# Gate-weight loads of an FFN asked for one unit earlier in a two-layer encoder trunk

## The chip, the cores and the metric

The kernel runs on one core of a Trainium2 chip. The metric is the device time of one execution in microseconds (us). The inputs and the output lie in HBM, and all arithmetic is float32, with each large operand split into a high and a low part.

## The reference

Two layers over 1024 rows of width 1024. Each layer is a token mixer (latent attention in layer 0, differential attention in layer 1) and a SwiGLU block, each followed by a layer norm over a scaled residual:

```
h = x
for i in range(DEPTH):                       # DEPTH = 2
    ...                                      # mix = attention of layer i
    h = layernorm(ALPHA * h + mix)
    gate, up = split(h @ w_gu[i])            # w_gu: 1024 x 5632
    h = layernorm(ALPHA * h + (silu(gate) * up) @ w_down[i])   # w_down: 2816 x 1024
```

The change lies in the first half of the SwiGLU block: the products of `h` with `w_gu`.

## The kernel before, in words

The function `ffn` is called once for each layer. Its first half multiplies the activations with the gate and up weights in 22 units (`NFF`) of one 128-column block of `w_gu` each. The two units of a pair (even and odd number) make the gate and the up half of one hidden block. A product of a unit is a 2x2 block product done with seven block multiplications instead of eight, named "1" to "7". So each unit needs sums and differences of its four weight blocks a11, a12, a21 and a22.

**A unit's weights.** `load(n)` asks the SP queue for the 1 MB of unit n (L563) into a tile `gr` of a pool of six large buffers (`big`). The same six buffers also hold `pg` (early results), `hp` and `sh` (hidden blocks on their way to HBM). `prepare(n, pr)` makes the operand of product `pr`: VectorE (DVE) forms the sums in place (L585: a21 += a22; L587: a11 = a21 - a11; L589: a12 -= a11; L593: a scratch tile `s`), ScalarE (ACT) casts to the high part (L514), and DVE or GpSimd (POOL) subtracts to get the low part (L515). The result is an operand tile `op_g` that TensorE (PE) reads.

**A unit's products.** `consume(n, pr)` issues 12 matmuls (L551) into a PSUM bank: `ga` for products 1 and 2, `gb` for 6, 7 and 4, `gc` for 5 and 3. Products 6, 7 and 4 of a unit add up in the same `gb` bank one after the other, and DVE reads the bank between them (L633 after 6, L637 after 7, L643 after 4). So the matmuls of product 7 wait for L633 of the same unit, and those of product 4 for L637. The rest (L635, L639, L641, L645) adds `gc`, and L663 and L664 multiply into `hp`. POOL then forms `sh` from `hp` (L668 to L671), and two stores (L674, L675) send both to HBM.

**Units 0 to 5** (`npre = 6`) are the units prepared in advance: their products 1 and 2 run early (`gates`, from a half-size load `gp`, L569), and the results `pg` of units 2 to 5 are stored to HBM (L682) and fetched back into `tmp` (L655) when the unit's other products run. Units 0 and 1 read `pg` directly, so that buffer is held until both are finished.

**Order.** The list `stream` names the (unit, product) steps; each turn prepares the step four places ahead and then consumes one. A unit's first `prepare` also asks for later units' weights (the lines that the change touches). A scheduler then fixes each engine's instruction order, and decides which of the six buffers each tile gets. Each engine works through its queue in that order and does not pass an instruction that waits. The SP queue holds the weight loads, the `pg` stores and fetches, and the `hp` and `sh` stores, in one order.

Below, (2,7) means product 7 of unit 2. In names such as `gr0_5`, the first number is the layer, the second the unit.

Of the kernel before, what the change touches and what calls it, by code (L numbers as in the profile page):

```python
# [42 lines left out]
def trunk(  # L43
# [66 lines left out]
    def big_tile(name, dt=F32R):  # L110
        return big.tile([P, 2, 1024], dt, tag="big", name=name)
# [396 lines left out]
    def op_unit(src, eng, name, tags=("wh", "wl"), pool=None):  # L508

        tag = tags[turns["op"] % len(tags)]  # L510
        turns["op"] += 1
        where = wp if tag in ("wh", "wl") else pool
        t = where.tile([P, 2, 512], F32R, tag=tag, name=f"op_{name}", bufs=6 if pool is where else 3)
        turns["hi"] = A.copy(t[:, 0], src).ins  # L514
        turns["last"] = eng.tensor_tensor(t[:, 1], src, f32(t[:, 0]), ALU.subtract).ins  # L515
        return t
# [4 lines left out]
    def ffn(side, xo, xst, pending, layer, x_src, x_dst, lng, lnb, next_x, spare=()):  # L521
# [15 lines left out]
        npre = 6  # L537
# [21 lines left out]
        def load(n):  # L559
            if n in r or n >= NFF:  # L560
                return
            r[n] = big_tile(f"gr{layer}_{n}", F32).rearrange("p a (b c) -> p (a b) c", b=2)
            nc.sync.dma_start(r[n], w_gu[layer, order[n]])  # L563
# [11 lines left out]
        def prepare(n, pr):  # L575


            if n not in begun:
                begun.add(n)
                load(n + 1)  # L580
                if n < npre - 1:
                    load(n + 2)
            a11, a12, a21, a22 = (r[n][:, i] for i in range(4))
            if pr == ("5" if n < 2 else "6"):
                V.tensor_tensor(a21, a21, a22, ALU.add)  # L585
            if pr == ("3" if n < 2 else "6"):
                V.tensor_tensor(a11, a21, a11, ALU.subtract)  # L587
            if pr == "3":
                V.tensor_tensor(a12, a12, a11, ALU.subtract)  # L589
            s3 = None  # L590
            if pr == "7":
                s3 = wp.tile([P, 2, 512], F32, tag="wr", name=f"s3_{layer}_{n}", bufs=2)[:, 0]
                V.tensor_tensor(s3, a22, a11, ALU.subtract)  # L593
            src, eng = {
                "1": (a11, G), "2": (a12, G), "6": (a11, V), "7": (s3, G), "5": (a21, V), "4": (a22, G),
                "3": (a12, V),
            }[pr]
            eng = V if n < 2 else eng
            ops[n, pr] = op_unit(src, eng, f"g{layer}_{n}_{pr}")
# [118 lines left out]
        for u in stream[:2]:  # L718
            prepare(*u)
# [3 lines left out]
        for u in stream[2:ahead]:  # L723
            prepare(*u)
# [4 lines left out]
        for i, u in enumerate(stream):  # L729
            if i + ahead < len(stream):  # L730
                prepare(*stream[i + ahead])
            consume(*u)
            if i % 5 == 0 and 40 <= i < 40 + 5 * len(spare):
                spare[i // 5 - 8]()
# [835 lines left out]
```

## Time and profile before

| what | us |
|---|---|
| three timed runs | 2275.31, 2277.39, 2277.57 |
| median | 2277.39 |
| profiled execution, its own time | 2276.84 |
| profiled execution, span from first to last instruction | 2275.1 |
| PE busy | 2238.8 (98% of the span) |
| DVE busy | 1569.9 (69%) |
| loads `gr<-in_w_gu` | 44 of 1 MB, median 6.8 from issue to landing |

A row of a timeline reads: start in us from the span's beginning, duration, engine, line, operation, names (output <- inputs, without numbers), shapes, count, and in brackets the idle time before it and what ended it. A row of waits reads: who waited, for whom, us in total, times, longest. A row of the chain of waits reads: start, duration, what. "DMA to landing" is the time from the issue of a transfer to its completion.

The stretches of interest are the starts of the main loop in the two layers: about 490 to 525 us in layer 0 and 1675 to 1710 us in layer 1.

### The profile page before, as it was taken

To read this page: it belongs to the slowest core of one execution; us is meant where nothing else is said; L and a number is where in the kernel's file an instruction comes from. 1 tells how busy PE (TensorE), PEld (TensorE's weight loads), DVE (VectorE), ACT (ScalarE), POOL (GpSimd) and SP (SyncE) were. 2 spreads that over 40 slices of the span, in tenths; PEclk is the share of its full clock that TensorE was granted. 3 is DMA by queue.
4 is the path that set the end of the run, shared out by engine and by line. 5 is a ranking of instruction groups with operands and counts; after the bars stand their busy time and mean duration, and the time that the engine had idled before them with its cause. 6 is when DMAs were issued, how large, how long until landed. Compare 5 with 4: busy or idle time off the path is not lost.

```text
span 2275.1 us, 31209 instructions
## 1 busy us (share of the span) xinstructions
PE 2238.8 (98%) x11410; PEld 1915.3 (84%) x11410; DVE 1569.9 (69%) x2848; ACT 1022.1 (45%) x2115; POOL 869.2 (38%) x693
## 2 busy tenths in 40 slices
PE   8999999999999999999999999999999999999998
PEld 8899998887888888888889898987778888888886
DVE  5676665696666667878576667677786656658878
ACT  4455664342333333445465656555432333334444
POOL 2232341113444444656333534322014444445551
PEclk9999999999999999999999999999999999999999
DMA  5010115443535338454311212054343223238453
GB/s 203 14 35 31 51 61 188 145 156 103 183 128 195 125 130 324 176 199 148 103 44 32 70 33 67 20 202 167 111 171 117 92 102 107 100 124 311 164 180 149
DMA packets 110443, 287.77 MB, mean 126 GB/s; under 512 B 8513, under 2 KB 30657, under 8 KB 99793
## 3 DMA queue, kind: packets, MB, share of 16 engines
q1 hardware_dynamic: 105872, 275.35, 34.2%
q0 software_dynamic: 4416, 10.42, 1.7%
q8 instruction: 90, 1.47, 0.3%
q14 instruction: 65, 0.52, 0.1%
HBM read 204.47 MB, written 77.07 MB: 124 GB/s over the span
## 4 chain that ended last, share of the span: by engine, by line
PE 87%; DVE 6%; DMA 3%; issue 2%; ACT 1%; POOL 1%; SPq 0%; DVEq 0%; POOLq 0%; ACTq 0%
PE gb L551 14%; PE gc L551 10%; PE ga L551 8%; PE dw L843 6%; PE zp_a L417 4%; PE s_a L219 4%; PE s_b L219 3%; PE dv L843 3%; PE bp L143 3%; PE bp L145 3%; PE dx L843 3%; PE bp L144 3%; PE dy L843 2%; PE o_a L262 2%; PE o_b L262 2%
## 5 line engine op out<-in xcount | busy, mean ns | idle before, releaser
L514 ACT CAST op_g<-gr 128x512 fp32r<-128x512 f32 x240 | 146.8, 621 | 378.6 <-PE gb L551 185.3
L515 POOL TENSOR_TENSOR op_g<-gr,op_g 128x512 fp32r<-128x512 f32 x104 | 145.7, 1406 | 248.7 <-ACT op_g L514 144.5
L515 DVE TENSOR_TENSOR op_h<-rh,op_h 128x512 fp32r<-128x512 f32 x152 | 169.5, 1144 | 48.3 <-ACT op_h L514 48.3
L551 PE MATMUL ga<-xh_m,op_g 128*128 128x512 f32 x512 | 168.3, 389 | 0.0
L514 ACT CAST op_h<-rh 128x512 fp32r<-128x512 f32 x152 | 92.6, 620 | 152.0 <-PE dx L843 50.4
L843 PE MATMUL dw<-op_w_t,op_h 128*128 128x512 f32 x660 | 151.6, 390 | 0.6 <-DVE op_h L515 0.6
L843 PEld LDWEIGHTS dw<-op_w_t,op_h 128*128 128x128 f32 x660 | 123.6, 188 | 26.8 <-DVE op_h L515 1.4
L515 POOL TENSOR_TENSOR op_w_t<-tt,op_w_t 128x512 fp32r<-128x512 f32 x66 | 101.8, 1551 | 84.5 <-ACT op_w_t L514 83.0
L227 ACT ACTIVATE l_b<-l_b,mx_b 128x256 f32<-128x256 f32 (+7 forms) x128 | 99.4, 777 | 66.8 <-DVE mx_b L222 65.3
L515 DVE TENSOR_TENSOR op_g<-gr,op_g 128x512 fp32r<-128x512 f32 x136 | 112.6, 832 | 16.9 <-ACT op_g L514 16.6
L515 POOL TENSOR_TENSOR op_g<-s,op_g 128x512 fp32r<-128x512 f32 x40 | 55.1, 1376 | 179.5 <-ACT op_g L514 171.4
L551 PE MATMUL gb<-t3h_f,op_g 128*128 128x512 f32 x352 | 117.9, 397 | 5.5 <-DVE tmp L633 5.5
L843 PE MATMUL dx<-op_w_b,op_h 128*128 128x512 f32 x528 | 121.1, 390 | 0.8 <-DVE op_w_b L515 0.8
L1367 POOL TENSOR_SCALAR l_b<-l_b,rb,cst 128x128 f32<-128x128 f32 (+3 forms) x64 | 52.6, 821 | 179.2 <-DVE rb L1366 171.8
L843 PEld LDWEIGHTS dx<-op_w_b,op_h 128*128 128x128 f32 x528 | 98.9, 188 | 22.4 <-DVE op_w_b L515 1.7
L551 PE MATMUL gb<-t4h_f,op_g 128*128 128x512 f32 x352 | 115.7, 390 | 1.3 <-DVE tmp L637 1.3
L551 PE MATMUL gc<-b22h_f,op_g 128*128 128x512 f32 x352 | 115.8, 390 | 0.8 <-DVE tmp L641 0.6
L551 PE MATMUL gb<-t2h_f,op_g 128*128 128x512 f32 x352 | 115.7, 390 | 0.4 <-DVE op_g L515 0.4
L551 PE MATMUL gc<-t1h_f,op_g 128*128 128x512 f32 x352 | 115.9, 390 | 0.0
L551 PEld LDWEIGHTS ga<-xh_m,op_g 128*128 128x128 f32 x512 | 96.2, 188 | 19.9
L143 PE MATMUL bp<-xT_f,h_wb 128*128 128x512 f32 x256 | 100.8, 394 | 0.1
L145 PE MATMUL bp<-xT_f,l_wb 128*128 128x512 f32 x256 | 100.7, 393 | 0.0
(391 smaller groups left out, 6753.5 us busy)
## 6 DMA issues: line engine op xcount, KB each, us to landing
gr<-in_w_gu SPq DMA_DIRECT2D x44, 1024.0 KB, 6.8
rh<-h_dr SPq DMA_DIRECT2D x28, 1024.0 KB, 4.9
h_dr<-sh SPq DMA_DIRECT2D x22, 1024.0 KB, 4.9
h_dr<-hp SPq DMA_DIRECT2D x22, 768.0 KB, 4.1
tt<-in_w_dn SPq DMA_DIRECT2D x44, 256.0 KB, 6.3
wo_dr<-op_pwo SPq DMA_DIRECT2D x16, 512.0 KB, 3.4
z<-xs_dr SPq DMA_DIRECT2D x16, 512.0 KB, 8.2
rw_b<-in_w_dn SPq DMA_DIRECT2D x8, 1024.0 KB, 7.7
```

Source lines behind the costliest of these rows:

```text
L143: T.matmul(ps_out, lh, rh, start=(i == 0), stop=False)
L144: T.matmul(ps_out, lh, rl, start=False, stop=False)
L145: T.matmul(ps_out, ll, rh, start=False, stop=(i == n - 1))
L219: T.matmul(s[:, :w], lh, rh[:, ks], start=(j == 0), stop=(j == len(q_pass) - 1))
L227: ends["exp"] = A.activation(l[:, :n], l[:, :n], AF.Exp, bias=mx, scale=-1.0, accum_out=sm).ins
L262: T.matmul(po[:, c], a, b[:, j % 2, c], start=st, stop=sp_, skip_group_check=True)
L417: T.matmul(m, a[:, h, :], self.wo[h][w][:, c], start=(start and h == heads[0] and a is oh and w == 0), stop=(stop and h == heads[-1] and a ...
L514: turns["hi"] = A.copy(t[:, 0], src).ins
L515: turns["last"] = eng.tensor_tensor(t[:, 1], src, f32(t[:, 0]), ALU.subtract).ins
L551: i = T.matmul(o, w[:, a, kc], x[b][:, k, :], start=(first and k == 0 and (a, b) == (0, 0)), stop=(k == 3 and a == 1), skip_group_check=Tr ...
L843: T.matmul(o, h[:, a, c], w[:, b_], start=(first and (a, b_) == (0, 0)), stop=(last and a == 1), skip_group_check=True,).ins for a, b_ in ...
L1367: G.tensor_scalar(l1[:, :n], l1[:, :n], r[:, 1:2], nlam, ALU.mult, ALU.mult)
```

## The change

When unit n is first prepared, the kernel before asks for unit n+1, and for n+2 while n is below 5. The kernel after asks for n+1 and n+2 always, and for n+3 while n is below 4.

```
             if n not in begun:
                 begun.add(n)
                 load(n + 1)
-                if n < npre - 1:
-                    load(n + 2)
+                load(n + 2)
+                if n < npre - 2:
+                    load(n + 3)
```

A unit already asked for isn't loaded again. So units 3 to 6 are now asked for when the unit three before them begins instead of two, and from unit 7 on each load is asked for two units ahead instead of one. The number of loads stays the same. After the change the kernel has one line more, so that L585 of before is L586 there, L633 is L634, L637 is L638, and so on.

Since each tile takes the buffer that the scheduler finds free, the places of the loads and the buffers move. On the SP queue in layer 0, before (from `gr0_3` on; `pg_dr` is the HBM copy of the early results):

```order
L563 DMA gr0_3_5604<-in_w_gu 128x2048
L563 DMA gr0_4_5736<-in_w_gu 128x2048
L682 DMA pg_dr0_5320<-pg0_4_5501 128x2048
L655 DMA tmp0_2_5830<-pg_dr0_5320 128x1024
L655 DMA tmp0_3_5925<-pg_dr0_5320 128x1024
L563 DMA gr0_5_5845<-in_w_gu 128x2048
L674 DMA h_dr0_0_5309<-hp0_0_5757 128x3x512
L675 DMA h_dr0_0_5309<-sh0_0_5818 128x4x512
L563 DMA gr0_6_5940<-in_w_gu 128x2048
```

And the same place now:

```order
L563 DMA gr0_3_5583<-in_w_gu 128x2048
L563 DMA gr0_4_5606<-in_w_gu 128x2048
L683 DMA pg_dr0_5320<-pg0_4_5501 128x2048
L563 DMA gr0_5_5738<-in_w_gu 128x2048
L656 DMA tmp0_2_5832<-pg_dr0_5320 128x1024
L656 DMA tmp0_3_5927<-pg_dr0_5320 128x1024
L675 DMA h_dr0_0_5309<-hp0_0_5759 128x3x512
L563 DMA gr0_6_5847<-in_w_gu 128x2048
L676 DMA h_dr0_0_5309<-sh0_0_5820 128x4x512
```

The load of unit 5 stands ahead of the two fetches of `tmp` and takes the buffer of `pg0_4` (released by that tile's store) instead of that of `gr0_2` (released by the last step of unit 2). The load of unit 6 stands one place earlier and takes the buffer of `pg0_0` instead of that of `hp0_0`.

On DVE in layer 0, before, from the reading of unit 1's bank on:

```order
L633 TENSOR_TENSOR tmp0_1_5766<-pg0_0_5321,gb0_1_5765 128x512
L635 TENSOR_TENSOR tmp0_1_5766<-tmp0_1_5766,gc0_15_5668 128x512
L635 TENSOR_TENSOR tmp0_1_5766<-tmp0_1_5766,gc0_13_5684 128x512
L593 TENSOR_TENSOR s3_0_4_5960<-gr0_4_5736 128x512
L637 TENSOR_TENSOR tmp0_0_5703<-pg0_0_5321,gb0_0_5702 128x512
```

The three sums of unit 5 follow twelve rows further on, before:

```order
L663 TENSOR_TENSOR hp0_0_5757<-pg0_0_5321 128x512
L585 TENSOR_TENSOR gr0_5_5845<-gr0_5_5845 128x512
L587 TENSOR_TENSOR gr0_5_5845<-gr0_5_5845 128x512
L589 TENSOR_TENSOR gr0_5_5845<-gr0_5_5845 128x512
L633 TENSOR_TENSOR tmp0_2_5830<-tmp0_2_5830,gb0_2_5829 128x512
```

And now, from the same reading of unit 1's bank on:

```order
L634 TENSOR_TENSOR tmp0_1_5768<-pg0_0_5321,gb0_1_5767 128x512
L586 TENSOR_TENSOR gr0_5_5738<-gr0_5_5738 128x512
L636 TENSOR_TENSOR tmp0_1_5768<-tmp0_1_5768,gc0_15_5670 128x512
L588 TENSOR_TENSOR gr0_5_5738<-gr0_5_5738 128x512
L594 TENSOR_TENSOR s3_0_4_5960<-gr0_4_5606 128x512
L636 TENSOR_TENSOR tmp0_1_5768<-tmp0_1_5768,gc0_13_5686 128x512
L638 TENSOR_TENSOR tmp0_0_5705<-pg0_0_5321,gb0_0_5704 128x512
L590 TENSOR_TENSOR gr0_5_5738<-gr0_5_5738 128x512
L640 TENSOR_TENSOR tmp0_0_5705<-tmp0_0_5705,gc0_05_5636 128x512
L638 TENSOR_TENSOR tmp0_1_5768<-pg0_0_5321,gb0_1_5767 128x512
L665 TENSOR_TENSOR hp0_0_5759<-tmp0_0_5705 128x512
L515 TENSOR_TENSOR op_g0_2_5_5784<-gr0_2_5581,op_g0_2_5_5784 128x512
```

The three sums of unit 5 have moved from just ahead of the first reading of unit 2's bank (`tmp0_2`) to between the readings of units 0 and 1. In layer 1 the first of them stands one place earlier still, ahead of the reading of unit 1's bank. The matmuls of PE stand in the same order as before up to the first ones of (5,5) in both layers.

## The prediction

> **What bounds the kernel now.** I read the page first, then the waits of PE, the chain of waits around the two starts of the main loop, and the timelines there.
>
> ```profile
> PE 2238.8 (98%) x11410; PEld 1915.3 (84%) x11410; DVE 1569.9 (69%) x2848; ACT 1022.1 (45%) x2115; POOL 869.2 (38%) x693
> PE gb L551 <- DVE tmp L633: 5.5, 2, 2.7
> PE gb L551 <- DVE tmp L637: 1.3, 1, 1.3
>   DVE gr L585: 17.5, 14
> ```
>
> PE is the bound: 2238.8 of 2275.1 us. A weight load that comes late costs time only where PE stands still for it. DVE waited 17.5 us, in 14 places, for `gr` loads (last row, from the view of the load's line), but the waits of PE behind DVE's readings are few. The largest are two of 2.7 us behind L633, one in each layer. The chain of waits, layer 0 first and then layer 1, tells what they hang on.
>
> ```profile
> 503.96 6.62 DMA gr<-in_w_gu
> 510.67 1.83 DVE gr L585
> ...
> 514.81 0.69 DVE tmp L633
> 515.54 4.61 PE gb L551 x12
> ...
> 520.61 2.74 PE gb L551 x12
> ...
> 1700.42 4.62 PE gb L551 x12
> ```
>
> The load of unit 5 is issued at 503.96 and lands at 510.58. DVE's three sums of that unit stand in the queue ahead of L633 of unit 2, and only that reading lets the matmuls of (2,7) start, at 515.54 after 2.74 us of idle time. So PE stands still for a unit that it needs much later: the load is late, and DVE does not pass it.
>
> The twelve matmuls after the stall take 4.61 us (4.62 in layer 1), while twelve take 2.74 us a little later. The windows show why: PE busy is the second figure of a row, the clock stands after POOL's entry.
>
> ```profile
> 513.11:516.53 3.42, 0.99 (x4) 0.85 (x5) 3.38 (x5) 0.35 (x1) 0.51 (x1) 1.00 1.05 353
> 516.53:519.94 3.41, 3.41 (x9) 2.66 (x9) 0.76 (x2) 0.00 (x0) 0.00 (x0) 0.50 0.14 58
> 844.18:847.59 3.41, 2.11 (x10) 1.43 (x9) 2.71 (x3) 1.07 (x2) 3.41 (x3) 1.00 0.49 191
> ```
>
> After a stretch with PE busy for 0.99 of 3.42 us the granted clock is 0.50 for the next 3.41 us. The stall of 1.3 us behind L637, with 2.11 of 3.41 us busy, kept the clock at 1.00. So each of the two stalls costs 2.74 us and then 4.61 - 2.74 = 1.87 us more: 4.6 us a layer, **9.2 us in all**. That is the most the change can win there.
>
> **The change part by part.** *The load of unit 5.* It no longer waits for the last step of unit 2. It now follows the `pg` store on the SP queue and needs only that store's end. The store and the `tmp` fetches in layer 0, and the store in layer 1; then the landing rows of the store of layer 0, of a load of layer 0 alone on the queues, and of the same two in layer 1. The last row is the window in which the new load would run in layer 0; its last two figures are the DMA share and the GB/s:
>
> ```profile
> 484.00 0.33 SPq L682 DMA_DIRECT2D pg_dr<-pg  x1
> 499.09 3.27 SPq L655 DMA_DIRECT2D tmp<-pg_dr  x2
> 1669.78 0.33 SPq L682 DMA_DIRECT2D pg_dr<-pg  x1
> DMA to landing us min/median/max: 5.9/5.9/5.9
> DMA to landing us min/median/max: 4.8/4.8/4.8
> DMA to landing us min/median/max: 4.3/4.3/4.3
> DMA to landing us min/median/max: 4.9/4.9/4.9
> 490.00:494.80 4.80, 4.80 (x23) 3.98 (x22) 4.02 (x7) 1.58 (x3) 0.19 (x1) 1.00 0.00 0
> ```
>
> Layer 0: 484.00 + 5.9 + 4.8 = 494.8 (rounded up for the issue). Layer 1: 1669.78 + 4.3 + 4.9 = 1679.0. The load's price is bounded below by 4.8 and above by the 6.62 of the row above. I take 4.8, since in that window nothing else moves. The `tmp` fetches now stand behind this load, but they went out at 499.09 at the earliest, 9 us after its issue, so nothing is lost there.
>
> *Where the three sums now stand.* They move into DVE's busiest stretch. Rows of DVE, POOL and PE there:
>
> ```profile
> 493.80 0.69 DVE L633 TENSOR_TENSOR tmp<-pg,gb 128x512 f32<-128x512 f32 x1
> 494.52 1.41 DVE L635 TENSOR_TENSOR tmp<-tmp,gc 128x512 f32<-128x512 f32 x2
> 496.54 0.68 DVE L637 TENSOR_TENSOR tmp<-pg,gb 128x512 f32<-128x512 f32 x1
> 499.95 0.69 DVE L515 TENSOR_TENSOR op_g<-gr,op_g 128x512 fp32r<-128x512 f32 x1
> 494.61 1.29 POOL L515 TENSOR_TENSOR op_g<-s,op_g 128x512 fp32r<-128x512 f32 x1 [45.60 <-ACT op_g L514]
> 497.22 1.29 POOL L515 TENSOR_TENSOR op_g<-gr,op_g 128x512 fp32r<-128x512 f32 x1 [1.32 <-ACT op_g L514]
> 510.65 1.29 POOL L515 TENSOR_TENSOR op_g<-s,op_g 128x512 fp32r<-128x512 f32 x1 [0.95 <-ACT op_g L514]
> 511.89 1.72 POOL L515 TENSOR_TENSOR op_g<-gr,op_g 128x512 fp32r<-128x512 f32 x1
> 499.04 0.39 PE L551 MATMUL gb<-t4h_f,op_g 128*128 128x512 f32 x1
> 501.76 0.39 PE L551 MATMUL gc<-t1h_f,op_g 128*128 128x512 f32 x1
> ```
>
> The deadlines are PE's: L637 of unit 0 must end before (0,4) starts at 499.04, and the L515 of `op_g` (2,5) before 501.76. Before, L637 ended at 497.22, so 1.8 us were to spare; the L515 ended at 500.64, 1.1 us to spare.
>
> An operation of DVE takes about 0.7 us alone. Beside POOL it can take longer: the L585 at 510.67 took 1.83 with a POOL operation from 510.65 to 511.94, that is, it ended 0.55 after POOL did. The POOL operation at 511.89 took 1.72 and ended 1.13 after DVE's. L635, which reads PSUM, took its usual 0.7 beside the POOL operation at 494.61. So I let a sum with both inputs in SBUF wait for POOL where POOL began first, and the reverse.
>
> This is what the Trainium skill, "SBUF — State Buffer", section "Who interferes with whom", states as a rule: a VectorE instruction with two SBUF inputs contends with a GpSimd instruction that reads SBUF, and the second to issue is blocked until the first ends. It speaks against this change; the trace agrees (1.83 instead of 0.69).
>
> Layer 0, in the new order: L633 ends at 494.49. L585 finds its load at 494.84, but POOL began at 494.61 and ends at 495.90, so L585 ends at 496.45. L635 to 497.1. L587 from 497.0 to 497.7, just ahead of POOL, which then ends at 498.8. L593 has two SBUF inputs too and ends at 499.4. L635 to 500.0, L637 to 500.65. So (0,4) starts 1.65 us late. Next L589, L639, L637 and L664 at about 0.65 each, and the L515 of (2,5) ends at 503.85. PE, now finishing (0,4) at 499.04 + 1.65 + 2.72 = 503.4, waits another 0.45. After that the three sums and the wait of 2.4 us ahead of them are gone from the place at 510.67: by the same steps L633 of unit 2 comes right behind (2,6), and PE runs from (3,6) into (2,7) without a stop. Layer 0 thus keeps 2.1 us of stalls.
>
> Layer 1, where L585 stands ahead of L633 of unit 1:
>
> ```profile
> 1677.21 1.40 DVE L635 TENSOR_TENSOR tmp<-tmp,gc 128x512 f32<-128x512 f32 x2
> 1679.37 1.29 POOL L515 TENSOR_TENSOR op_g<-s,op_g 128x512 fp32r<-128x512 f32 x1 [49.20 <-ACT op_g L514]
> 1682.15 1.30 POOL L515 TENSOR_TENSOR op_g<-gr,op_g 128x512 fp32r<-128x512 f32 x1 [1.48 <-issue]
> 1683.91 0.39 PE L551 MATMUL gb<-t4h_f,op_g 128*128 128x512 f32 x1
> ```
>
> DVE is free at 1678.6, the load is there at 1679.1, ahead of POOL. But L587 then waits for POOL to 1681.45, L593 for the next POOL operation to 1683.8, and now all three sums stand ahead of L637 of unit 0, which ends at 1685.05 instead of being due at 1683.91: 1.15 us late. The L515 of (2,5) adds 0.55. Layer 1 keeps 1.7 us.
>
> Sum: -9.2 + 2.1 + 1.7 = **-5.4 us**. Bounds: with no waiting for POOL at all, L637 meets both deadlines and only some 0.3 us a layer is left at (2,5): -8.6 us. With the load at 6.6 instead of 4.8, it is about 1 us more in each layer and nearer -3. If a new stall halves the clock, add 1.87 for each. By the busy shares above, 1.3 us of idle time did not and 2.74 did; 1.65 lies between, nearer to the first, so I take no halving.
>
> The Trainium skill, "TensorE: Matmul & The Clock Gate", section "What's actually happening", gives an idle window of about 3.4 us as the condition for the halved clock; by that rule no new stall here would meet it, the sum stays -5.4, and the halving in rival (b) below would fall away. The trace disagrees with it, as 2.74 us of idle time was enough.
>
> *The load of unit 6* now takes the buffer of `pg` of units 0 and 1. It goes out once that is read for the last time (L663) and the `hp` store ahead of it is issued. The last reading, and the start of (2,4) on PE:
>
> ```profile
> 507.58 0.68 DVE L663 TENSOR_TENSOR hp<-pg 128x512 f32<-128x512 f32 x1
> 525.23 0.39 PE L551 MATMUL gb<-t4h_f,op_g 128*128 128x512 f32 x1
> ```
>
> By the steps above that reading ends about 3 us later than before, at 511.3, and the load, at 6.62 as beside other transfers, lands near 518.5. Its L585 now stands ahead of L637 of unit 2, on which (2,4) hangs. PE stopped at 515.54 - 2.74 = 512.80 before; with 2.1 us of stalls (2,7) starts at 514.9, and (2,4) follows after 525.23 - 515.54 - 1.87 = 7.8 us, at 522.7. The two DVE operations need 1.4 us. So some 2.8 us cover this wait; a load later than that stops PE.
>
> *All later loads* stand on SP where the load of the unit before stood, and so do their L585 on DVE. The waits of the 17.5 us row stay and are hidden, as now. I take nothing for them.
>
> **The rivals.** (a) *Everything goes.* The new sums fit in between without PE seeing it: the load lands 0.25 us earlier, L585 goes ahead of POOL, and (0,4) is not late. Layer 0 then keeps 0.45; the like in layer 1 gives -8.6, or 2268.8. For it: the margin is small. Against: three sums of 0.7 go into 1.8 us of slack. Chance 0.2.
>
> (b) *The stall moves and stays large.* The load takes 6 us or more, or a 1.65 us stall halves the clock in one or both layers: -5.4 + 1.9 to 3.8, that is 2273.9 to 2275.8. For it: the wait is for a transfer again, in front of the same queue. Chance 0.35.
>
> (c) *Slower.* Each later load now takes a buffer that must first be free, two units ahead. If the SP queue stands still at it, the stores and fetches behind it come late, and DVE stands in front of L633 or L637 for them. There are 16 units from 6 on in each layer, 32 in all. At 0.31 us of PE idle time in each, 10 us, the time comes to 2282.0 and is slower; from there it decides, and at 0.5 us each it is 2288. Against: the 14 waits of DVE now, 1.25 us each, stopped PE twice only. Chance 0.05.
>
> (d) *The change doesn't do what it says*: the load is moved on SP but lands as late. It can't, unless the `pg` store is 9 us late. Below 0.02, counted in (b).
>
> **How the numbers follow.** The profiled execution took 2276.84, with 2275.1 of span and 1.74 around it. Less 5.4 that is 2271.4; the median of the runs, 2277.39, lies 0.55 above the profiled execution, so the forecast is **2272.0**, with a chance of 0.4. The range reaches from 2268.0 (the whole 9.2 won is 2268.2) to 2276.6 (nearly all of it given back), and leaves out some 0.15. A measurement tells 0.2%, 4.6 us, from no change. So faster is a win of more than 4.6: (a) whole, 0.35 of the forecast's 0.4 and 0.02 of (b), together 0.57. Slower is 0.04 of (c). The rest, 0.39, is the same.
>
> **What would show it.** Right: no idle time of 2.7 us behind L633; `gr` of unit 5 issued near 490 and 1674; L585 in the middle of L633 to L637; idle time of 1 to 2 us ahead of (0,4) behind L637, and under 0.6 ahead of (2,5); clock 1.00 throughout both stretches. Wrong: a stall of over 2 us in either place, a clock of 0.50 there, or new waits of PE behind `gr` in the units from 6 on.

## The result, and the profile after

| what | before | after |
|---|---|---|
| median, us | 2276.02 (6 runs, 2273.64 to 2277.57) | 2269.95 (6 runs, 2266.45 to 2272.97) |
| profiled execution, us | 2276.84 | 2268.81 |
| span, us | 2275.1 | 2267.0 |

The ratio after to before is 0.9973, with a 95% interval of 0.996 to 0.9986: 6.1 us less, where 5.4 were forecast.

The engines' row of the page of the changed kernel, the waits of PE and the idle time ahead of the first sum (the L585 of before is L586 now):

```profile
PE 2234.0 (99%) x11410; PEld 1911.9 (84%) x11410; DVE 1563.6 (69%) x2848; ACT 1022.1 (45%) x2115; POOL 875.1 (39%) x693
```

```profile
PE gb L551 <- DVE tmp L638: 3.3, 3, 1.3
```

```profile
  DMA gr<-in_w_gu: 14.2, 10
```

The two waits of 2.7 us behind the reading of unit 2's bank are gone. What is left of this kind is behind L638, three times, at most 1.3 us. DVE still waits 14.2 us for `gr` loads, against 17.5 before: most of those waits are still there, and what went is the place of two of them.

The chain of waits of the changed kernel in layer 0 names nothing but PE:

```profile
507.61 2.72 PE gb L551 x12
...
510.56 5.44 PE gb L551 x24
```

The 24 matmuls from 510.56 are (3,6) and (2,7) in one piece. Before, 2.74 us of idle time and twelve matmuls of 4.61 us stood here. Now the timeline of layer 0, with rows of SP, DVE, POOL and PE:

```profile
484.47 0.33 SPq L683 DMA_DIRECT2D pg_dr<-pg  x1
490.17 0.33 SPq L563 DMA_DIRECT2D gr<-in_w_gu  x1
...
494.27 0.69 DVE L634 TENSOR_TENSOR tmp<-pg,gb 128x512 f32<-128x512 f32 x1
494.91 0.69 DVE L586 TENSOR_TENSOR gr<-gr 128x512 f32<-128x512 f32 x1
...
496.12 1.19 DVE L588 TENSOR_TENSOR gr<-gr 128x512 f32<-128x512 f32 x1
497.23 0.68 DVE L594 TENSOR_TENSOR s<-gr 128x512 f32<-128x512 f32 x1
...
498.43 0.67 DVE L638 TENSOR_TENSOR tmp<-pg,gb 128x512 f32<-128x512 f32 x1
499.02 0.68 DVE L590 TENSOR_TENSOR gr<-gr 128x512 f32<-128x512 f32 x1
...
517.91 0.69 DVE L586 TENSOR_TENSOR gr<-gr 128x512 f32<-128x512 f32 x1 [2.47 <-DMA gr<-in_w_gu]
518.52 0.68 DVE L638 TENSOR_TENSOR tmp<-tmp,gb 128x512 f32<-128x512 f32 x1
...
495.08 1.67 POOL L515 TENSOR_TENSOR op_g<-s,op_g 128x512 fp32r<-128x512 f32 x1 [45.04 <-ACT op_g L514]
...
499.51 0.39 PE L551 MATMUL gb<-t4h_f,op_g 128*128 128x512 f32 x1
...
521.05 0.39 PE L551 MATMUL gb<-t4h_f,op_g 128*128 128x512 f32 x1
```

The load goes out at 490.17, 13.8 us earlier than before. The L586 begins at 494.91, 0.17 us ahead of POOL's operation at 495.08, and takes 0.69. L638 of unit 0 ends at 499.10, and (0,4) starts at 499.51 with no idle time. The rows from 517.91 on are the first sum of unit 6, unit 2's reading behind it and (2,4). In layer 1 it is closer:

```profile
1674.61 1.19 DVE L588 TENSOR_TENSOR gr<-gr 128x512 f32<-128x512 f32 x1
...
1676.93 1.78 DVE L590 TENSOR_TENSOR gr<-gr 128x512 f32<-128x512 f32 x1
1678.63 0.67 DVE L638 TENSOR_TENSOR tmp<-pg,gb 128x512 f32<-128x512 f32 x1
...
1679.36 0.50 PE L551 MATMUL gb<-t4h_f,op_g 128*128 128x512 f32 x1 [0.93 <-DVE tmp L638]
```

Here two of the three sums take 1.19 and 1.78 beside POOL, and all three stand ahead of L638. So 0.93 us of idle time is left ahead of (0,4).

### The profile page after: what moved, and what is told of

The parts are those of the page before. It is cut to its first block, busy times and chain, and to the rows that moved or that the text cites. A ratio compares the mean times of both kernels' runs of the same rounds, so it can differ in the third digit from the quotient of the medians.

```text
span 2267.0 us, 31215 instructions
## 1 busy us (share of the span) xinstructions
PE 2234.0 (99%) x11410; PEld 1911.9 (84%) x11410; DVE 1563.6 (69%) x2848; ACT 1022.1 (45%) x2115; POOL 875.1 (39%) x693
## 4 chain that ended last, share of the span: by engine, by line
PE 89%; DVE 5%; DMA 3%; issue 1%; ACT 1%; POOL 0%; SPq 0%; DVEq 0%; POOLq 0%; ACTq 0%
PE gb L551 15%; PE gc L551 10%; PE ga L551 9%; PE dw L844 6%; PE zp_a L417 4%; PE s_a L219 4%; PE s_b L219 3%; PE dx L844 3%; PE dv L844 3%; PE bp L143 3%; PE bp L145 3%; PE bp L144 3%; PE dy L844 3%; PE o_a L262 2%; PE o_b L262 2%; PE hq L1061 1%
## 5 line engine op out<-in xcount | busy, mean ns | idle before, releaser
L515 POOL TENSOR_TENSOR op_g<-gr,op_g 128x512 fp32r<-128x512 f32 x104 | 145.6, 1404 | 251.3 <-ACT op_g L514 134.8
L515 DVE TENSOR_TENSOR op_h<-rh,op_h 128x512 fp32r<-128x512 f32 x152 | 168.3, 1135 | 48.4 <-ACT op_h L514 48.4
L515 POOL TENSOR_TENSOR op_w_t<-tt,op_w_t 128x512 fp32r<-128x512 f32 x66 | 102.2, 1557 | 84.1 <-ACT op_w_t L514 84.0
L515 DVE TENSOR_TENSOR op_g<-gr,op_g 128x512 fp32r<-128x512 f32 x136 | 114.6, 846 | 19.1 <-ACT op_g L514 18.9
L515 POOL TENSOR_TENSOR op_g<-s,op_g 128x512 fp32r<-128x512 f32 x40 | 57.5, 1437 | 164.2 <-ACT op_g L514 156.2
```

## The experiments

The theory (A in the expectations): the gain is the wait for unit 5's load, taken out of DVE's queue ahead of the reading on which (2,7) hangs. The chief rival (B): the loads two units ahead in the rest of the main loop carry it. The runs below were timed in three sets, each beside its own runs of the kernel before; the medians of the three sets of before were 2275.68 (19 runs), 2276.12 (24) and 2276.41 (10).

| kernel | set | median, us | ratio to before, 95% interval |
|---|---|---|---|
| three ahead only | 1 | 2269.56 | 0.9971 (0.9959 to 0.9982) |
| two ahead only | 1 | 2274.06 | 0.9993 (0.9984 to 1.0002) |
| late load, sums moved back | 1 | 2267.96 | 0.9966 (0.9953 to 0.9978) |
| changed, first sum one place later | 1 | 2269.81 | 0.9974 (0.9963 to 0.9984) |
| changed, sums behind unit 0's reading | 2 | 2269.82 | 0.9973 (0.9963 to 0.9983) |
| three ahead always | 2 | 2269.35 | 0.9973 (0.9963 to 0.9983) |
| late load, two places | 2 | 2269.00 | 0.9971 (0.9961 to 0.9981) |
| changed, again | 2 | 2270.51 | 0.9976 (0.9967 to 0.9985) |
| early load, sums moved back | 3 | 2269.41 | 0.9967 (0.9954 to 0.9979) |
| late load, sums moved back, again | 3 | 2269.87 | 0.9971 (0.9958 to 0.9984) |

**Three ahead only.** One half of the change:

```
                 if n < npre - 1:
                     load(n + 2)
+                if n < npre - 2:
+                    load(n + 3)
```

> Kernel before plus the load three units ahead (n below 4) alone; the loads of units 7 and later stay one ahead. Theory A (the gain is the earlier load of unit 5, which takes a wait out of DVE's queue): the whole gain is here, 5 to 7 us less than before (ratio 0.997 to 0.998, near 2270); no idle time of PE at (2,7) in either layer, about 0.9 us left ahead of (0,4) in layer 1, as in the changed kernel. Rival B (the loads two ahead in the main loop carry the gain): within 1.5 us of before, near 2276, though the two stalls are gone. On the clock, in this and the other runs of the set: the stall of about 2.05 us near 1625 to 1630, which no edit touches, is followed by half clock in some profiles and not in others if fixed windows of 3.41 us decide; if the length of the stall decides, it is the same in all.

It won 6.1 us, all that the whole change wins. Neither layer has idle time at (2,7); 0.93 us is left ahead of (0,4) in layer 1:

```profile
1681.59 0.50 PE L551 MATMUL gb<-t4h_f,op_g 128*128 128x512 f32 x1 [0.93 <-DVE tmp L639]
```

**Two ahead only.** The other half:

```
-                if n < npre - 1:
-                    load(n + 2)
+                load(n + 2)
```

> Kernel before with the loads two units ahead always, and none three ahead, so that the load of unit 5 stands where it stood. Theory A: no gain, 2276 within 1.5 us (ratio 0.9993 to 1.0007); both stalls of 2.7 us ahead of (2,7) stay, behind the reading of unit 2's bank. Rival B: 5 to 7 us less than before. Rival C (SP stands still at a later load for its buffer, and what stands behind it comes late): 1 us or more slower, with new idle time of PE in units 6 and later.

Its interval takes in no change, and the waits of PE show the same two stalls:

```profile
PE gb L551 <- DVE tmp L632: 5.5, 2, 2.7
```

The chain of waits of this kernel in layer 0:

```profile
503.53 7.12 DMA gr<-in_w_gu
...
510.74 1.32 DVE gr L584
...
514.37 0.69 DVE tmp L632
...
515.11 3.01 PE gb L551 x12
```

Load, sums and reading stand in a row as they did before. Rival B, with its 5 to 7 us, falls. The median is 1.6 us below that of before, and 0.4 us outside the 1.5 that theory A allowed. Its mean granted clock over 11 runs is 0.9972 against 0.9965 over 19, and 0.0007 of 2275 us is 1.6 us, so I put no more to it than the clock, though the interval doesn't exclude a small gain. The last row shows the clock at work: twelve matmuls took 3.01 us here after the same stall, where they took 4.61 before.

**Late load, sums moved back.** The loads and the whole SP order of before; on DVE, unit 5's first sum stays behind the first reading of unit 2's bank:

```
             if pr == ("5" if n < 2 else "6"):
-                V.tensor_tensor(a21, a21, a22, ALU.add)
+                i = V.tensor_tensor(a21, a21, a22, ALU.add).ins
+                if n == 5:
+                    behind(i, ends["u2", 2])
...
             if pr == "6":
-                V.tensor_tensor(u2, p1, acc[n, "b"], ALU.add)
+                ends["u2", n] = V.tensor_tensor(u2, p1, acc[n, "b"], ALU.add).ins
```

> Kernel before with all its loads and the whole SP order as they were; the first sum of unit 5 alone is kept behind the first reading of unit 2's bank on DVE. Theory A (the late load costs only because DVE's queue stands behind it): the load still lands near 510.6 and 1696 or so, the two stalls ahead of (2,7) fall from 2.74 to under 0.5 us, no half clock there, and 6 to 9 us are won, as much as by the change or more, since no sum moves into DVE's busiest stretch and (0,4) isn't late. Rival D (the late weights themselves, or the transfers beside them, hold PE up): the stall comes back at the next product, and the time stays within 1.5 us of 2276.

> The kernel with the late load, and the first sum of unit 5 behind the first reading of unit 2's bank, once more: beside the run before this one it shows whether the early load counts once the sums stand out of the way. Theory A: 2267 to 2270, ratio to before 0.9955 to 0.9975, the same within 1 us as the run before; stalls ahead of (2,7) of some 0.26 again. Rival H: 1.5 us or more above the run before.

The chain of waits of the first of these two runs:

```profile
504.20 6.65 DMA gr<-in_w_gu
...
510.94 1.78 DVE gr L585
...
512.75 1.68 DVE gr L589
...
515.82 0.61 DVE tmp L635
...
516.47 3.06 PE gb L551 x12
```

And the stall that is left, in its timeline:

```profile
516.47 0.51 PE L551 MATMUL gb<-t3h_f,op_g 128*128 128x512 f32 x1 [0.26 <-DVE tmp L635]
```

The load is as late as before (504.20 to 510.85) and the sums wait for it just as long. The stall falls from 2.74 to 0.26 us in both layers, now ahead of (3,7) and not of (2,7), as the second expectation has it, since only unit 3's reading is left behind the sums. The time falls by 7.7 us and, in set 3, by 6.5. This shows the step on which the whole prediction rests: the late load cost nothing by itself, the order of DVE's queue did.

**Early load, sums moved back.** The same edit on the changed kernel.

> Changed kernel, its early load kept, with the first sum of unit 5 kept behind the first reading of unit 2's bank on DVE: the sums then stand neither ahead of that reading nor among the readings of units 0 and 1. Theory A: no stall ahead of (0,4) in either layer in any case of who is first on DVE and POOL, none above 0.5 ahead of (2,7) or (3,7); 0.5 to 2 us less than the changed kernel, near 2268.7, and the same within 1 us as the kernel with the late load and the same place of the sums, since then the time of the load counts for nothing. Rival H (an early load is worth something by itself): 1.5 us or more less than that kernel.

2269.41 beside 2269.87 for the late load with the same place of the sums: no difference can be told, and nothing speaks for rival H. But these are five and six runs that scatter over 2.7 and 4.7 us, so the 1.5 us of rival H aren't excluded either. Its profile has no idle time of PE above 0.22 us at the start of the main loop of either layer. All the same its time can't be told from that of the changed kernel, since the intervals of the ratios overlap; the 0.5 to 2 us that were expected between them aren't shown.

**Changed, first sum one place later.** On the changed kernel:

```
             if pr == ("5" if n < 2 else "6"):
-                V.tensor_tensor(a21, a21, a22, ALU.add)
+                i = V.tensor_tensor(a21, a21, a22, ALU.add).ins
+                if n == 5:
+                    behind(i, ends["u2", 1, True])
...
-                    V.tensor_tensor(u2, u2, c, ALU.add)
+                    ends["u2", n, c is acc[n, "cs"][0]] = V.tensor_tensor(u2, u2, c, ALU.add).ins
```

> Changed kernel with the first sum of unit 5 kept one place later on DVE, behind the first addition of a second bank to unit 1's result; its load stays early. It then begins behind the POOL operation near 495.1 instead of ahead of it. Step of the prediction (a sum with two inputs in SBUF that begins second waits until POOL has ended and 0.55 us more): the sum takes about 1.8 us instead of 0.7, the reading of unit 0's bank ends 1 to 1.8 us past the time at which (0,4) could start in layer 0, and the time is 1 to 2 us above the changed kernel, near 2271.5. Rival E (the place among the POOL operations does not matter): no stall ahead of (0,4) in layer 0 and the time of the changed kernel, 2270. In layer 1 the stall of 0.9 us ahead of (0,4) stays within 0.7 by both.

The timeline of its layer 0:

```profile
494.75 1.32 DVE L586 TENSOR_TENSOR gr<-gr 128x512 f32<-128x512 f32 x1
...
497.19 1.78 DVE L590 TENSOR_TENSOR gr<-gr 128x512 f32<-128x512 f32 x1
498.89 0.68 DVE L640 TENSOR_TENSOR tmp<-pg,gb 128x512 f32<-128x512 f32 x1
...
494.23 1.29 POOL L515 TENSOR_TENSOR op_g<-s,op_g 128x512 fp32r<-128x512 f32 x1 [44.99 <-ACT op_g L514]
496.84 1.58 POOL L515 TENSOR_TENSOR op_g<-gr,op_g 128x512 fp32r<-128x512 f32 x1 [1.32 <-ACT op_g L514]
...
499.62 0.50 PE L551 MATMUL gb<-t4h_f,op_g 128*128 128x512 f32 x1 [0.80 <-DVE tmp L640]
```

POOL ends at 495.52 and the sum at 496.07; POOL ends at 498.42 and the next sum at 498.97: 0.55 us later both times, as the prediction had it. A stall of 0.80 stands ahead of (0,4), where the first profile of the changed kernel had none; it is less than the 1 to 1.8 expected, since POOL was 0.5 us into its operation when the first sum began. The wait for POOL is shown by these rows. The 2271.5 that was expected didn't come: in the median, 2269.81, so small a stall can't be told. Nor does the 0.80 show what the edit costs, since the changed kernel itself can have a stall in this place, as the next run shows.

**Changed, again.** No edit.

> The changed kernel once more, beside the other three. All theories: 2268.5 to 2271.5, and the stall of 0.9 us ahead of (0,4) in layer 1 again, none at (2,7). On the clock: the stall of 2.05 us near 1624 is followed by half clock or not, as it falls in the windows of 3.41 us: followed by half clock if PE is busy for under 0.42 of the window, not if for over 0.45.

The time came as expected, the stalls didn't: 0.9 us ahead of (0,4) in layer 1 alone was named. This profile of the same kernel showed what the first one had hidden. Its layer 0:

```profile
493.26 1.74 DVE L586 TENSOR_TENSOR gr<-gr 128x512 f32<-128x512 f32 x1 [0.21 <-DMA gr<-in_w_gu]
494.92 0.67 DVE L636 TENSOR_TENSOR tmp<-tmp,gc 128x512 f32<-128x512 f32 x1
495.52 0.68 DVE L588 TENSOR_TENSOR gr<-gr 128x512 f32<-128x512 f32 x1
496.12 1.77 DVE L594 TENSOR_TENSOR s<-gr 128x512 f32<-128x512 f32 x1
...
493.17 1.28 POOL L515 TENSOR_TENSOR op_g<-s,op_g 128x512 fp32r<-128x512 f32 x1 [44.49 <-ACT op_g L514]
...
499.15 0.50 PE L551 MATMUL gb<-t4h_f,op_g 128*128 128x512 f32 x1 [1.39 <-DVE tmp L638]
```

L586, held until its load was there, began 0.09 us after POOL had begun instead of 0.17 us ahead of it. So L586 and L594 took 1.74 and 1.77, and (0,4) started 1.39 us late: the prediction's own steps, one by one, and nearly its 1.65. In layer 1 L586 came 0.03 us after POOL (1674.15 and 1674.12) and took 1.81; it stands ahead of unit 1's reading there, so 0.60 us of idle time came up ahead of (1,7), which no term of the sum had, and 0.45 was left ahead of (0,4).

**Changed, sums behind unit 0's reading.** The three sums kept behind L638 of unit 0, by a `behind` like the ones above.

> Changed kernel with the early load kept, and the three sums of unit 5 kept behind the first reading of unit 0's bank for product 7 on DVE. Theory A: the 0.93 us ahead of (0,4) in layer 1 goes, since nothing of unit 5 stands ahead of the reading that (0,4) hangs on, and no stall comes back at (2,5) above 0.4; 0.5 to 1 us less than the changed kernel, near 2269, 6.5 to 7.5 less than before. Rival F (the sums cost the same wherever they stand in that stretch): the stall moves to (2,5) or (1,4) with 0.9 us or more, and the time is that of the changed kernel, 2270.

The 0.93 ahead of (0,4) is gone, but 0.39 and 0.38 come up ahead of (2,7): one operation of unit 5 (`s`, L594 of the changed kernel) now stands ahead of unit 2's reading and takes 1.76 beside POOL. 2269.82 beside 2270.51 of the changed kernel in the same set is the size expected, and within the scatter.

**Three ahead always.** `load(n + 3)` without the condition.

> Changed kernel with the load three units ahead for all units, so that every load from unit 7 on waits on SP for a buffer one unit longer. Theory A: the time of the changed kernel within 1.5 us (2270), with the same start of the main loop, since the later loads are covered. Rival C of the prediction (SP stands still for a buffer, the stores and fetches behind it come late, 0.3 us or more of PE idle time in each of 32 units): 10 us or more above the changed kernel, 2280; if it decides in a few units only, 2 us or more and new idle time of PE there.

2269.35: no loss. One stall is new beside the changed kernel, 0.45 us behind POOL at 743.4; the other later units have none that the changed kernel lacks. Rival C, the prediction's slower case, falls.

**Late load, two places.** The late load with the sums moved back, and the low half of unit 21's product 6 kept behind the reading of unit 20:

```
             ops[n, pr] = op_unit(src, eng, f"g{layer}_{n}_{pr}")
+            if (n, pr) == (NFF - 1, "6"):
+                behind(turns["last"], ends["u3", n - 1])
```

> Kernel before with all its loads as they were, the first sum of unit 5 kept behind the first reading of unit 2's bank on DVE as in the earlier run, and the low half of unit 21's product 6 kept behind the reading of unit 20's bank on which (20,4) hangs. Theory A (PE waits there for DVE's order, and the order alone mends it): the 1.3 us near 841 and the 0.6 to 1.1 us near 2024 go, 1.3 to 2.4 us less than the run with the one place, near 2266.3, and ratio 0.995 to 0.9965 to before. Rival G (a reading of PSUM beside a POOL operation waits as well, or the low half is then late for product 6 of unit 21): the stall stays or moves to the next product, and the time is 2268.

I missed this one: 2269.0, not 2266.3. The timeline shows where:

```profile
841.84 0.69 DVE L641 TENSOR_TENSOR tmp<-tmp,gb 128x512 f32<-128x512 f32 x1 [1.19 <-PE gb L551]
...
841.42 0.39 PE L551 MATMUL gb<-t3h_f,op_g 128*128 128x512 f32 x1
842.68 0.47 PE L551 MATMUL gb<-t4h_f,op_g 128*128 128x512 f32 x1 [0.87 <-DVE tmp L641]
```

DVE is now idle ahead of the reading and starts it as soon as PE is done, yet PE stands still for 0.87 us. (20,7) and (20,4) use the same bank one right behind the other, so 0.87 is what such a reading costs here with nothing ahead of it, and only 0.4 of the 1.3 was DVE's order. In layer 1 the stall was ahead of product 3, 0.64 us behind DVE, in the run with the one place; it is still there, now 0.82 us behind ACT: rival G.

## Why the prediction was right, point by point

**The bound and what the stalls hang on: right.** Late load, sums moved back, against two ahead only, shows it.

**The new load's landing: right.** Layer 0: 490.17 to 494.88, 4.71 from the issue, where 4.8 and 494.8 were taken. Layer 1: the `pg` store goes out at 1664.13 and the load lands at 1673.18, 9.05 us later, where 4.3 + 4.9 = 9.2 was taken.

**The stalls that stay: the mechanism right, the size too large, and this is the term that failed.** Predicted were 2.1 us in layer 0 and 1.7 in layer 1. The first profile of the changed kernel has 0 and 0.93, the second 1.39 and 1.05. The step that failed reads "L585 finds its load at 494.84, but POOL began at 494.61": a margin of 0.23 us, worked out from the rows of one execution, was taken as settled. It is a race that either side wins: L586 began 0.17 us ahead of POOL in one execution and 0.09 behind it in the other. Rival (a) happened in layer 0 of the first, the forecast's case in the second. The mean of the two, (0.93 + 2.44) / 2 = 1.7 us, is 2.1 less than the 3.8 of the sum. That the median, too, is 2.05 below the forecast is chance: 1.37 of it is the kernel before, forecast from 2277.39 (three runs) and then measured at 2276.02 (six). The gain itself is off by 0.7 only, 6.1 against 5.4.

**The stalls at (2,5), 0.45 and 0.55: wrong, none was there in either profile.** Five operations lead from the end of unit 0's reading to the end of the L515 of (2,5). The sum gave them 3.2 us (500.65 to 503.85); in the run again they took 3.0 (499.10 to 502.10), for they start 0.60 apart (498.43, then 499.02 in the timeline of layer 0) though each is shown with 0.68. And the twelve matmuls of (0,4) took 3.01 right after their stall, where 2.72 was taken. The two together make up the 0.45.

**What the two old stalls cost, 4.6 a layer and so 9.2 at most: right for the profiled execution, too large as a mean.** Twelve matmuls after a stall of 2.74 without half clock took 3.01 (two ahead only). So of the 1.87 the half clock makes 4.61 - 3.01 = 1.6. The other 0.27 goes with any such stall, those that stay too (3.01 after the 1.39 above), and nearly drops out of the sum. The half clock also doesn't come in every execution. The mean granted clock of 24 runs of before is 0.9963, of 11 of the changed kernel beside them 0.9975; 0.0012 of 2272 us is an estimated 2.8 us of clock, not 3.7. With it the sum is -5.5 + 1.7 - 2.8 = -6.6; measured were 6.1 in the result and 5.6 in the set with the kernel again. The rest, 0.5 to 1 us, is no more than these medians scatter. So two terms were too large, one for the change and one against it, and that they partly cancel is luck: the forecast gain came out nearer than its terms.

**No halving by the stalls that stay: right, for a wrong reason.** Neither 0.93 nor 1.39 halved the clock, but length isn't what decides (next section but one).

**The load of unit 6: covered, with less to spare.** It took 7.61 from its issue at 510.20, not 6.62. DVE waited 2.47 us for it. L638 of unit 2 ended at 519.20, and (2,4) came at 521.05: 1.85 us of cover, not 2.8.

**All later loads, nothing: right within the scatter of the times**, by two ahead only and three ahead always. The profiles do show one price, at unit 20 of layer 1. All seven profiles with the later loads two or more ahead have 1.07 us of idle time there, ahead of (20,4), which in them stands right behind (20,7). In the kernel before, in three ahead only and in both runs of late load, sums moved back, product 5 stands between the two, and the idle time is 0.64, ahead of product 3. The 0.4 us between them is in no term of the sum. The profiled kernel has one more thing that I didn't foresee, small stalls of 0.25 to 0.31 near 1650, but they come and go between executions and I can't put them to the change.

**Contention with POOL.** The Trainium skill, "SBUF — State Buffer", section "Who interferes with whom", says that the later of the two waits until the earlier has ended. 1.74, 1.32 and 1.78 in place of 0.69, each ending 0.55 after POOL, agree with it.

## What to carry to other kernels

When PE waits for a reading on another engine, look at what stands ahead of that reading in the engine's queue and waits for a transfer; it can be mended by loading earlier or by moving the waiting work back, and here no difference between the two could be told. A forecast that hangs on which of two operations begins first, with some 0.2 us between them, should carry both outcomes with their chances. Two products that use one bank in turn, one right behind the other, paid 0.87 us for the reading here with nothing ahead of it, so moving DVE's work could shorten that stall only to this.

## What the runs showed of the hardware that I had not expected

The granted clock is decided in fixed windows of 3.41 us, and a stall counts by how it falls into them. All half-clock stretches in a profile start whole multiples of 3.413 us apart: in before at 516.53, 1632.69 and 1700.95, which is 327 and 20 windows. The stall of 2.74 us in layer 0 of two ahead only fell across two windows, and the clock stayed at 1.00; that of layer 1 filled one and was followed by 0.50 (PE busy is the second figure of a row; the clock stands after POOL's entry):

```profile
509.83:513.24 3.41, 2.54 (x12) 1.76 (x10) 2.47 (x2) 1.44 (x3) 2.97 (x2) 1.00 1.04 406
513.24:516.65 3.41, 1.54 (x7) 1.29 (x8) 3.38 (x6) 0.00 (x0) 0.00 (x0) 1.00 0.85 302
516.65:520.06 3.41, 3.41 (x17) 2.83 (x16) 2.09 (x4) 0.62 (x1) 0.00 (x0) 1.00 0.09 34
1694.25:1697.67 3.42, 0.68 (x4) 0.26 (x2) 3.35 (x5) 0.62 (x1) 1.40 (x1) 1.00 1.03 344
1697.67:1701.08 3.41, 3.41 (x8) 2.65 (x9) 1.65 (x3) 0.00 (x0) 0.00 (x0) 0.50 0.42 173
```

A stall of some 2.05 us at the start of layer 1's feed-forward, which no edit touches, shows the same between two executions of the changed kernel. The first profile, and then the run again:

```profile
1624.37:1627.78 3.41, 1.78 (x12) 1.64 (x13) 2.58 (x3) 1.45 (x4) 0.26 (x1) 1.00 1.00 363
1627.78:1631.19 3.41, 3.41 (x17) 2.79 (x16) 1.70 (x3) 3.41 (x8) 0.00 (x0) 1.00 0.93 347
```

```profile
1622.85:1626.26 3.41, 1.35 (x7) 0.81 (x6) 2.97 (x5) 1.59 (x3) 0.93 (x1) 1.00 0.89 269
1626.26:1629.67 3.41, 3.41 (x13) 3.02 (x14) 1.81 (x3) 1.50 (x3) 0.00 (x0) 0.50 0.97 390
```

With PE busy for 1.78 of 3.41 us the clock stayed, with 1.35 it was halved; in two ahead only 1.54 didn't halve it. So the bound in these stretches lies between 0.40 and 0.45 of a window. In all, this stall halved the clock in seven of the twelve profiles. In the attention of layer 1, where the matmuls are of other kinds, a window with more busy time than that was followed by half clock, here in three ahead only:

```profile
1494.74:1498.15 3.41, 1.62 (x9) 1.12 (x9) 3.35 (x8) 0.54 (x3) 0.27 (x1) 1.00 1.04 429
1498.15:1501.56 3.41, 3.28 (x8) 1.99 (x8) 2.54 (x9) 2.90 (x7) 0.26 (x1) 0.50 1.00 423
```

So the bound isn't one figure for all work, and what it counts there stays open.

The Trainium skill, "TensorE: Matmul & The Clock Gate", section "What's actually happening", says that the window runs freely and that an idle window of about 3.4 us brings half clock. The runs agree with the first; against the second, a window with 0.40 of it busy was enough. About 1.6 us of the 8.0 between the two profiled executions is thus no work of the change: the stall near 1630 halved the clock in the one of before and not in that of after.
